# Where the tiles of an encoder trunk begin in SBUF: small tiles first, large tiles at multiples of 256 bytes

## The chip, the cores and the metric

The kernel runs on one core of a Trainium2 chip. The metric is the device time of one execution in microseconds (us). Before the change the median of three runs is 1626.02 us (1625.46 to 1627.36).

## What is computed

One layer of a bidirectional encoder on 256 rows (tokens) of 2048 channels, all in float32. A combined input projection feeds a gated short convolution and a grouped-query attention (16 query heads, 4 key/value heads of 128 channels, two-dimensional rotary positions); both are projected, gated, merged and projected once more. Then comes a squared-ReLU MLP with 8192 hidden channels. RMS norms stand before and after each half.

```python
h = rmsnorm(x, norm_mix_pre[l])
z = h @ w_in[l]
conv_b, conv_c, conv_in, q, k, v, g_a, g_b = jnp.split(z, IN_OFFSETS, axis=-1)
y_a = short_conv_mixer(conv_b, conv_c, conv_in, conv_w[l], w_out_conv[l])
...
y_b = block_gqa(q, k, v) @ w_out_attn[l]
...
mixed = (gate_a * y_a + gate_b * y_b) @ w_merge[l]
x = x + rmsnorm(mixed, norm_mix_post[l])
h = rmsnorm(x, norm_mlp_pre[l])
f = jnp.square(jax.nn.relu(h @ w_up[l])) @ w_down[l]
x = x + rmsnorm(f, norm_mlp_post[l])
```

## The kernel before

Almost all the work is matrix products of the 256 activations with weight matrices that are read once from HBM. A weight matrix is cut into blocks of 512 columns; a block is read in granules of two K tiles (128 partitions x 2 x 512 float32, 512 KB, tile `raw`, queue SP, L121). `split` (L72) turns a granule into two fp32r tiles: ScalarE rounds it (`whi`, L75), VectorE subtracts that from the original (`wlo`, L76). The activations lie split in the same way in SBUF: `pair` (L83) makes one tile `A`, `B` or `C` of 32 KB in each partition that holds the rounded part and the remainder, 16 K tiles of 256 rows each. Three matmuls then make one product: high x high, one part's high with the other's remainder, and the reverse.

There are two forms of the product:

- `linear_channels` (L161): the weights are stationary (128 columns of `whi` or `wlo`), the activations move, 256 columns a matmul (L175, L179, L182). A granule has 24 matmuls. The gated convolution, the gates, both branch projections and 15 of the 16 up-projection blocks run so.
- `linear` (L133): the activations are stationary, the weights move, 512 columns a matmul (L145, L146, L147). A granule has 12 matmuls. K, V, the four Q blocks, the merge, the first up-projection block and the whole down projection run so.

Attention proper (L377 to L379) uses the same triple of 256 columns: scores have `qh` or `ql` stationary and `kh`/`kl` (tile `kv`) moving; values have `vh`/`vl` (tile `kv`) stationary and the probabilities `ph`/`pl` moving. TensorE also transposes (L224, L410, L575), with the 128x128 identity `ident` moving.

The order of the work is written out by hand: small pieces are put off by a number of granules (`later`, `tick`). The granules of one block follow each other without a gap in the program.

Two rings hold `whi` and `wlo`. While attention and convolution run (up to about 450 us) there is the pool `wts` alone, four tiles of each. After that the pool `wts2` takes the place of the mixing stage's tiles, and `weights` (L113) changes between the rings every four granules:

```python
pool = rings[count[0] // WB % len(rings)]
count[0] += 1
```

A pool takes a consecutive piece of each partition in the order in which the pools are opened (L61 to L70), and each tile in it a place that is rounded up to 32 bytes. Before the change the small tiles of `const` (1184 bytes) come first, then `big`, `wts`, `wk`, the small tiles of `sm` (704 bytes), and last the pool of the mixing stage, whose place `wts2` and `late` take over. The start of each tile in its partition, in bytes:

```
tiles                                  before          start modulo 256
ident                                  16512           128
A / kv, m, mg / C / B      17696, 50464, 66848, 99616   32
raw, whi, wlo of wts               132384 to 181535     32
bias, cc (and what shares its place)   181536 ...       32
mixing stage: ph, pl, qh, ql, z, ra    190432 ...      224
whi, wlo of wts2                       190432 ...      224
```

Rows, K tiles and column blocks inside these tiles are 512, 1024 or 2048 bytes apart, so every operand of a matmul begins at the same remainder as its tile.

Of the kernel before, what the change touches and what calls it, by code (L numbers as in the profile page):

```python
# [9 lines left out]
F32 = mybir.dt.float32  # L10
# [5 lines left out]
P = 128  # L16
D = 2048
T = 256
NT = T // P
# [13 lines left out]
def trunk_kernel(  # L33
# [16 lines left out]
    nc = tc.nc  # L50
# [8 lines left out]
    WARM = 9  # L59

    const = ctx.enter_context(tc.tile_pool(name="const", bufs=1))  # L61
    big = ctx.enter_context(tc.tile_pool(name="big", bufs=1))
    wts = ctx.enter_context(tc.tile_pool(name="wts", bufs=WB))
    wk = ctx.enter_context(tc.tile_pool(name="wk", bufs=2))
    sm = ctx.enter_context(tc.tile_pool(name="sm", bufs=2))
    ps_acc = ctx.enter_context(tc.tile_pool(name="ps_acc", bufs=4, space=bass.MemoryType.PSUM))
    ps_tr = ctx.enter_context(tc.tile_pool(name="ps_tr", bufs=2, space=bass.MemoryType.PSUM))
    ps_at = ctx.enter_context(tc.tile_pool(name="ps_at", bufs=2, space=bass.MemoryType.PSUM))
# [64 lines left out]
    def linear(act, wv, done, k0=0, k1=KT, lag=0, ahead=None):  # L133

        ah, al, _ = act
        accs = [ps_acc.tile([P, CH], F32, name="acc") for _ in range(NT)]

        def step(t, k, wh, wl):  # L140
            ts_ = slice(t * P, (t + 1) * P)
            for g in range(KG):
                a = k - k0 + g
                first, last = a == 0, a == k1 - k0 - 1
                nc.tensor.matmul(accs[t], lhsT=ah[:, a, ts_], rhs=wh[:, g, :], start=first, stop=False)  # L145
                nc.tensor.matmul(accs[t], lhsT=ah[:, a, ts_], rhs=wl[:, g, :], start=False, stop=False)  # L146
                nc.tensor.matmul(accs[t], lhsT=al[:, a, ts_], rhs=wh[:, g, :], start=False, stop=last)  # L147
            if k + KG == k1:
                done(t, accs[t])

        behind = []
        for gran in weights(wv, k0, k1, ahead):
            behind.append(gran)
            step(0, *gran)
            if len(behind) > lag:
                step(1, *behind.pop(0))
            tick()
        for gran in behind:
            step(1, *gran)
# [42 lines left out]
    def along_rows(dst, cols):  # L202

        rb = ps_at.tile([P, T], F32, name="at")
        ones = wk.tile([P, P], F32, tag="cc", bufs=CCB, name="ones")
        nc.vector.memset(ones, 1.0)
        for t in range(NT):
            diag = wk.tile([P, P], F32, tag="cc", bufs=CCB, name="diag")
            nc.vector.tensor_scalar_mul(diag, ident, cols[t])
            nc.tensor.matmul(rb[:, t * P : (t + 1) * P], lhsT=ones, rhs=diag, start=True, stop=True)  # L210
        nc.vector.tensor_copy(dst, rb)
# [20 lines left out]
    def rsqrt_mean(dst, ss, n):  # L232

        ms = sm.tile(list(ss.shape), F32, name="ms")
        nc.vector.tensor_scalar(ms, ss, 1.0 / n, EPS, op0=ALU.mult, op1=ALU.add)
        nc.gpsimd.tensor_tensor(dst, ms, mhalf.broadcast_to(list(ss.shape)), op=ALU.pow)  # L236

    def row_squares(dst, src):

        junk = wk.tile([P, CH], F32, tag="cc", bufs=CCB, name="junk")  # L240
        nc.scalar.activation(junk, src, AF.Square, accum_out=dst)

    def total(dst, parts):

        s = sm.tile([P, NT], F32, name="tot")
        nc.vector.tensor_reduce(s, parts, axis=AX.X, op=ALU.add)
        rsqrt_mean(dst, s, D)
# [10 lines left out]
        nc.scalar.activation(act, zero[:, :1], AF.Square)  # L258
    ident = const.tile([P, P], F32, name="ident")
    make_identity(nc, ident)  # L260
    mhalf = const.tile([P, 1], F32, name="mhalf")
    nc.vector.memset(mhalf, -0.5)
    ch = const.tile([P, 7, KT], F32, name="ch")
    nc.scalar.dma_start(ch, chan)
    g_pre, g_mlp, cw = ch[:, 0, :], ch[:, 1, :], ch[:, 2:5, :]
# [7 lines left out]
        for i in range(n):  # L273
            split(xt[:, i, :], hT[0][:, k + i, :], hT[1][:, k + i, :], scale=g_pre[:, k + i : k + i + 1])

    rstd = const.tile([P, NT], F32, name="rstd")
    norm_row = wk.tile([P, 2, T], F32, name="bias", bufs=1)
    xv = x.rearrange("(t p) d -> p t d", p=P)
    tabs = [mx.tile([P, 2, NT, HD], F32, name=f"tab{i}", bufs=1) for i in range(2)]

    def norm_in():

        ss0 = const.tile([P, NT, 4], F32, name="ss0")
        for j in range(4):
            xj = mx.tile([P, NT, CH], F32, tag="t4", bufs=4, name="xj")
            nc.sync.dma_start(xj, xv[:, :, j * CH : (j + 1) * CH])
            for t in range(NT):
                row_squares(ss0[:, t, j : j + 1], xj[:, t, :])
        total(rstd, ss0)
        along_rows(norm_row[:, 0, :], [rstd[:, t : t + 1] for t in range(NT)])  # L290
        nc.vector.tensor_tensor(norm_row[:, 1, :], norm_row[:, 0, :], norm_row[:, 0, :], op=ALU.mult)
# [71 lines left out]
    kl = kv[:, 1]  # L363
    later(9, tables)
    later(11, norm_in)
    head_norm_rope(w_in[C_K], tabs[1], kh, kl, 7, wait=6, ahead=first_operands)
    vh = kv[:, 2].rearrange("p a b -> p (a b)").rearrange("p (t c) -> p t c", t=NT)
# [160 lines left out]
    def gain_row(r):  # L528
        g = wk.tile([P, CH], F32, name="bias", bufs=1)
        nc.scalar.dma_start(g, rows[r : r + 1, :].partition_broadcast(P))  # L530
        return g
# [1 line left out]
    rows1 = const.tile([P, 6], F32, name="rows1")  # L533

    def row_rsqrt(parts, t, at):
        s = sm.tile([P, 1], F32, name="s1")
        nc.vector.tensor_reduce(s, parts[:, t, :], axis=AX.X, op=ALU.add)
        r = rows1[:, at : at + 1]
        rsqrt_mean(r, s, D)
        return r  # L540


    ss1 = const.tile([P, NT, 4], F32, name="ss1")
    ss2 = const.tile([P, NT, 4], F32, name="ss2")
    xr = big.tile([P, 2, NT, D], F32, tag="A", name="xr")[:, 0]
    nc.scalar.dma_start(xr, xv)
# [18 lines left out]
    def residual(t, x2):  # L565
        r = row_rsqrt(ss1, t, t)
        ts_ = slice(t * P, (t + 1) * P)
        for c in range(4):
            cs = slice(c * CH, (c + 1) * CH)
            nc.vector.scalar_tensor_tensor(x2[:, t, cs], x2[:, t, cs], r, xr[:, t, cs], op0=ALU.mult, op1=ALU.add)  # L570
            pool, name = bank(c)
            tr = pool.tile([P, 4, P], F32, name=name)
            for i in range(4):
                d = c * 4 + i
                nc.tensor.transpose(tr[:, i, :], x2[:, t, d * P : (d + 1) * P], ident)  # L575
            ds = slice(c * 4, c * 4 + 4)
            n = wk.tile([P, 4, P], F32, tag="cc", bufs=CCB, name="cc")
            nc.vector.tensor_tensor(n, tr, g_mlp[:, ds].unsqueeze(2).broadcast_to([P, 4, P]), op=ALU.mult)
            split(n, x2T[0][:, ds, ts_], x2T[1][:, ds, ts_])
# [8 lines left out]
    def norms():  # L588
        for t in range(NT):
            for j in range(4):  # L590
                row_squares(ss2[:, t, j : j + 1], x2[:, t, j * CH : (j + 1) * CH])
            rstd2[t] = row_rsqrt(ss2, t, 2 + t)
        along_rows(rstd2_row, rstd2)
# [36 lines left out]
    before = [None] * NT  # L630

    def finish(t, last):
        ms = sm.tile([P, 1], F32, name="ms3")
        nc.vector.scalar_tensor_tensor(ms, ss3[:, t, 3:4], 1.0 / D, before[t], op0=ALU.mult, op1=ALU.add)
        r = sm.tile([P, 1], F32, name="rs3")
        nc.gpsimd.tensor_tensor(r, ms, mhalf, op=ALU.pow)
        for c in range(4):
            js = slice(c * CH, (c + 1) * CH)
            f = facc[:, t, js] if c < 3 else last
            nc.vector.scalar_tensor_tensor(x2[:, t, js], f, r, x2[:, t, js], op0=ALU.mult, op1=ALU.add)  # L640
            nc.sync.dma_start(outv[:, t, js], x2[:, t, js])

    def down(q, j, fT):
        js = slice(j * CH, (j + 1) * CH)
        g = gain_row(4 + j) if q == 3 else None

        def done(t, acc):
            fj = facc[:, t, js]
            if q == 0:
                nc.scalar.copy(fj, acc)  # L650
                return
            nc.vector.tensor_tensor(fj, acc, fj, op=ALU.add)
            if q < 3:
                return
            row_squares(ss3[:, t, j : j + 1], fj)
            if j < 3:
                nc.vector.tensor_tensor(fj, fj, g, op=ALU.mult)
            else:
                last = wk.tile([P, CH], F32, tag="cc", bufs=CCB, name="cc")
                nc.vector.tensor_tensor(last, fj, g, op=ALU.mult)  # L660
                finish(t, last)
            if j == 2:
                s = sm.tile([P, 1], F32, name="s1")
                nc.vector.tensor_reduce(s, ss3[:, t, :3], axis=AX.X, op=ALU.add)
                before[t] = rows1[:, 4 + t : 5 + t]
                nc.vector.tensor_scalar(before[t], s, 1.0 / D, EPS, op0=ALU.mult, op1=ALU.add)

        linear(fT, w_dn[j], done, q * KT, (q + 1) * KT, lag=LAG if q == 3 and j == 3 else 0)
# [71 lines left out]
```

## Time and profile before

| what | value |
|---|---|
| median of three runs | 1626.02 us (1625.46 to 1627.36) |
| the profiled execution, its own time | 1625.61 us |
| its span, from first to last instruction | 1623.8 us |
| TensorE matmul busy | 1610.9 us, 99% of the span |
| VectorE, ScalarE, GpSimd busy | 947.5, 709.5, 35.6 us |
| read from HBM | 302.44 MB, 188 GB/s over the span |

The profile is one execution taken by the hardware profiler. The span is cut into 40 slices for a row of digits that gives busy shares in tenths. A matmul's duration in the trace runs from its start to its end through the array, and neighbours overlap; what a matmul costs in a row of them is the distance from one start to the next. The view by stretches counts every instruction that is under way in the stretch, so at its edges it counts one to three more than begin in it.

### The profile page before, as it was taken

The page shows a single profiled execution, that of the slowest core. Times are in us where ns is not written, and L with a number is a line of the kernel's source. Part 1 is how long each engine was busy: PE and PEld are TensorE (multiplying, and loading weights), DVE is VectorE, ACT ScalarE, POOL GpSimd, SP SyncE. Part 2 cuts the span into 40 slices and gives each one's busy share as a digit, 9 for nine tenths or more (in the row PEclk, how much of TensorE's full clock was granted, in tenths as well). Part 3 has the DMA queues.
Part 4 walks back from the last instruction along what each step waited for, and adds up shares of the span by engine and source line. Part 5 has one row for each costly group of instructions (what it writes and reads, how often), then busy time and mean ns, then how long its engine had stood idle before and what let it go on. Part 6 is the DMA issues. An engine that isn't in the chain of part 4 may idle for free.

```text
span 1623.8 us, 26863 instructions
## 1 busy us (share of the span) xinstructions
PE 1610.9 (99%) x11210; PEld 1497.9 (92%) x11210; DVE 947.5 (58%) x1107; ACT 709.5 (44%) x860; POOL 35.6 (2%) x23
## 2 busy tenths in 40 slices
PE   9999999999999999999999999999999999999997
PEld 7899999999999999999988898889988998899986
DVE  6767676576764544555554865446654565555654
ACT  7444444444454443444444644444433344333441
POOL 0210101001000000000000000000000000000000
PEclk9999999999999999999999999999999999999999
DMA  8654545555475556565765566555565565556562
GB/s 317 204 177 156 181 147 181 181 167 183 149 241 186 186 188 194 186 190 184 243 204 177 172 209 195 189 187 189 185 197 189 187 190 189 193 182 195 191 200 83
DMA packets 86297, 306.28 MB, mean 189 GB/s; under 512 B 9632, under 2 KB 10016, under 8 KB 85920
## 3 DMA queue, kind: packets, MB, share of 16 engines
q1 hardware_dynamic: 84608, 300.32, 57.2%
q10 hardware_dynamic: 1568, 4.25, 0.8%
q8 instruction: 87, 1.43, 0.4%
q14 instruction: 34, 0.28, 0.1%
HBM read 302.44 MB, written 2.10 MB: 188 GB/s over the span
## 4 chain that ended last, share of the span: by engine, by line
PE 97%; DVE 1%; issue 1%; DMA 0%; POOL 0%; ACT 0%; SPq 0%; DVEq 0%; POOLq 0%; ACTq 0%
PE acc L182 20%; PE acc L175 20%; PE acc L179 20%; PE acc L146 12%; PE acc L147 12%; PE acc L145 12%; PE at L377 0%; PE at L379 0%; PE at L378 0%; PE tr L410 0%; DMA raw<-in_w_in 0%; PE tr L224 0%; POOL rs L236 0%; DVE wlo L76 0%; PE tr L575 0%
## 5 line engine op out<-in xcount | busy, mean ns | idle before, releaser
L76 DVE TENSOR_TENSOR wlo<-raw,whi 128x1024 fp32r<-128x1024 f32 (+1 forms) x561 | 684.2, 1221 | 602.8 <-ACT whi L75 590.9
L75 ACT CAST whi<-raw 128x1024 fp32r<-128x1024 f32 (+1 forms) x561 | 587.1, 1048 | 774.2 <-PE acc L179 401.6
L175 PE MATMUL acc<-A,whi 128*128 128x256 f32 x1280 | 362.3, 283 | 0.0
L182 PE MATMUL acc<-A,wlo 128*128 128x256 f32 x1280 | 360.4, 282 | 0.0
L179 PE MATMUL acc<-A,whi 128*128 128x256 f32 x1280 | 360.3, 282 | 0.0
L175 PE MATMUL acc<-C,whi 128*128 128x256 f32 x1216 | 340.0, 280 | 0.0
L182 PE MATMUL acc<-C,wlo 128*128 128x256 f32 x1216 | 339.9, 280 | 0.0
L179 PE MATMUL acc<-C,whi 128*128 128x256 f32 x1216 | 339.9, 279 | 0.0
L145 PE MATMUL acc<-whi,A 128*128 128x512 f32 x704 | 275.0, 392 | 2.2 <-ACT whi L75 2.2
L146 PE MATMUL acc<-wlo,A 128*128 128x512 f32 x704 | 275.9, 392 | 1.0 <-DVE wlo L76 1.0
L147 PE MATMUL acc<-whi,A 128*128 128x512 f32 x704 | 275.3, 391 | 0.0
L179 PEld LDWEIGHTS acc<-A,whi 128*128 128x128 f32 x1280 | 244.4, 191 | 0.2
L175 PEld LDWEIGHTS acc<-A,whi 128*128 128x128 f32 x1280 | 244.4, 191 | 0.2
L182 PEld LDWEIGHTS acc<-A,wlo 128*128 128x128 f32 x1280 | 244.5, 191 | 0.0
L175 PEld LDWEIGHTS acc<-C,whi 128*128 128x128 f32 x1216 | 230.8, 190 | 0.2
L179 PEld LDWEIGHTS acc<-C,whi 128*128 128x128 f32 x1216 | 230.8, 190 | 0.2
L182 PEld LDWEIGHTS acc<-C,wlo 128*128 128x128 f32 x1216 | 230.8, 190 | 0.0
L145 PEld LDWEIGHTS acc<-whi,A 128*128 128x128 f32 x704 | 131.8, 188 | 32.1 <-ACT whi L75 3.1
L146 PEld LDWEIGHTS acc<-wlo,A 128*128 128x128 f32 x704 | 132.0, 187 | 31.9 <-DVE wlo L76 2.7
L147 PEld LDWEIGHTS acc<-whi,A 128*128 128x128 f32 x704 | 132.0, 187 | 29.0
L182 PE MATMUL acc<-B,wlo 128*128 128x256 f32 x256 | 71.6, 280 | 0.0
L179 PE MATMUL acc<-B,whi 128*128 128x256 f32 x256 | 71.6, 280 | 0.0
(144 smaller groups left out, 1115.6 us busy)
## 6 DMA issues: line engine op xcount, KB each, us to landing
raw<-in_w_in SPq DMA_DIRECT2D x207, 512.0 KB, 4.3
raw<-in_w_up SPq DMA_DIRECT2D x128, 512.0 KB, 3.5
raw<-in_w_dn SPq DMA_DIRECT2D x128, 512.0 KB, 3.4
raw<-in_w_oc SPq DMA_DIRECT2D x32, 512.0 KB, 4.4
raw<-in_w_oa SPq DMA_DIRECT2D x32, 512.0 KB, 4.3
raw<-in_w_mg SPq DMA_DIRECT2D x32, 512.0 KB, 4.1
xj<-in_x SPq DMA_DIRECT2D x4, 512.0 KB, 9.0
xr<-in_x ACTq DMA_DIRECT2D x1, 2048.0 KB, 9.7
```

The costliest lines, as they stand in the source:

```text
L75: nc.scalar.copy(hi, src)
L76: nc.vector.tensor_tensor(lo, src, hi.bitcast(F32), op=ALU.subtract)
L145: nc.tensor.matmul(accs[t], lhsT=ah[:, a, ts_], rhs=wh[:, g, :], start=first, stop=False)
L146: nc.tensor.matmul(accs[t], lhsT=ah[:, a, ts_], rhs=wl[:, g, :], start=False, stop=False)
L147: nc.tensor.matmul(accs[t], lhsT=al[:, a, ts_], rhs=wh[:, g, :], start=False, stop=last)
L175: nc.tensor.matmul(acc, lhsT=wh[:, g, cs], rhs=ah[:, a, :], start=a == 0 and c % 2 == 0, stop=False, skip_group_check=True,)
L179: nc.tensor.matmul(acc, lhsT=wh[:, g, cs], rhs=al[:, a, :], start=False, stop=False, skip_group_check=True)
L182: nc.tensor.matmul(acc, lhsT=wl[:, g, cs], rhs=ah[:, a, :], start=False, stop=a == KT - 1, skip_group_check=True)
```

## The change

The pool `sm` is opened right after `const`, ahead of `big`. Some small tiles are merged or share a place: `ss0` and `ss1` become halves of `ss01`, `mhalf` and `rstd` columns of `half`, and `s1`, `ms3`, `rs3` take turns in the places of `rden`, `ms`, `rs`. The small tiles then end at byte 18176, which is 71 x 256; all later tiles are multiples of 256 bytes long. So `A` begins at 18176, `kv` at 50944, `C` at 67328, `B` at 100096, `raw` at 132864, the `whi`/`wlo` of `wts` at 149248 and on, and the mixing stage's tiles and `wts2` at 190208: all at remainder 0. `ident` stays at 16512.

```diff
     const = ctx.enter_context(tc.tile_pool(name="const", bufs=1))
+
+    sm = ctx.enter_context(tc.tile_pool(name="sm", bufs=2))
     big = ctx.enter_context(tc.tile_pool(name="big", bufs=1))
     wts = ctx.enter_context(tc.tile_pool(name="wts", bufs=WB))
     wk = ctx.enter_context(tc.tile_pool(name="wk", bufs=2))
-    sm = ctx.enter_context(tc.tile_pool(name="sm", bufs=2))
...
-    mhalf = const.tile([P, 1], F32, name="mhalf")
-    nc.vector.memset(mhalf, -0.5)
+    ss01 = const.tile([P, 2, NT, 4], F32, name="ss01")
+    half = const.tile([P, 4], F32, name="half")
+    nc.vector.memset(half, -0.5)
+    mhalf = half[:, :1]
+    rstd = half[:, 2:4]
...
-    rstd = const.tile([P, NT], F32, name="rstd")
...
-        ss0 = const.tile([P, NT, 4], F32, name="ss0")
+        ss0 = ss01[:, 0]
...
-        s = sm.tile([P, 1], F32, name="s1")
+        s = sm.tile([P, 1], F32, tag="rden", name="s1")
...
-    ss1 = const.tile([P, NT, 4], F32, name="ss1")
+    ss1 = ss01[:, 1]
...
-        ms = sm.tile([P, 1], F32, name="ms3")
+        ms = sm.tile([P, 1], F32, tag="ms", name="ms3")
...
-        r = sm.tile([P, 1], F32, name="rs3")
+        r = sm.tile([P, 1], F32, tag="rs", name="rs3")
...
-                s = sm.tile([P, 1], F32, name="s1")
+                s = sm.tile([P, 1], F32, tag="rden", name="s1")
```

No instruction moves: on every engine the same instructions stand in the same order, with the same waits on all but GpSimd. GpSimd has one more wait ahead of each of its last two instructions (L636 before, in `finish`).

## Rows read from the trace of the kernel before

**Rows 1.** The page: busy time by engine, the slices of TensorE and its clock.
```profile
PE 1610.9 (99%) x11210; PEld 1497.9 (92%) x11210; DVE 947.5 (58%) x1107; ACT 709.5 (44%) x860; POOL 35.6 (2%) x23
PE   9999999999999999999999999999999999999997
...
PEclk9999999999999999999999999999999999999999
```

**Rows 2.** The page: the chain that ended last, share of the span by engine.
```profile
PE 97%; DVE 1%; issue 1%; DMA 0%; POOL 0%; ACT 0%; SPq 0%; DVEq 0%; POOLq 0%; ACTq 0%
```

**Rows 3.** Groups by line and shape: line, engine, operation, tiles, count, busy us, mean ns.
```profile
L175 PE MATMUL acc<-A,whi 128*128 128x256 f32 x1280 | 362.3, 283 | 0.0
L175 PE MATMUL acc<-C,whi 128*128 128x256 f32 x1216 | 340.0, 280 | 0.0
L175 PE MATMUL acc<-B,whi 128*128 128x256 f32 x256 | 71.6, 280 | 0.0
...
L145 PE MATMUL acc<-whi,A 128*128 128x512 f32 x704 | 275.0, 392 | 2.2 <-ACT whi L75 2.2
L145 PE MATMUL acc<-whi,B 128*128 128x512 f32 x128 | 50.2, 392 | 0.0
L145 PE MATMUL acc<-whi,C 128*128 128x512 f32 x32 | 12.5, 396 | 0.0
L410 PE MATMUL tr<-ident,pr 128*128 128x128 f32 x64 | 9.6, 273 | 0.0
```

**Rows 4.** Timeline of TensorE where a ring of weights ends: start us, us, instruction.
```profile
461.97 0.28 PE L175 MATMUL acc<-A,whi 128*128 128x256 f32 x1
462.09 0.28 PE L179 MATMUL acc<-A,whi 128*128 128x256 f32 x1
462.21 0.28 PE L182 MATMUL acc<-A,wlo 128*128 128x256 f32 x1
462.33 0.28 PE L175 MATMUL acc<-A,whi 128*128 128x256 f32 x1
462.44 0.28 PE L179 MATMUL acc<-A,whi 128*128 128x256 f32 x1
462.56 0.28 PE L182 MATMUL acc<-A,wlo 128*128 128x256 f32 x1
462.67 0.28 PE L175 MATMUL acc<-A,whi 128*128 128x256 f32 x1
```

**Rows 5.** TensorE by stretches: us, busy (count), granted clock, DMA share, GB/s.
```profile
139.43:153.81 14.38, 14.38 (x122) 1.00 0.73 239
153.81:175.60 21.79, 21.79 (x99) 1.00 0.60 191
462.33:473.21 10.88, 10.88 (x98) 1.00 0.81 272
473.21:484.73 11.52, 11.52 (x98) 1.00 0.70 241
1003.78:1014.98 11.20, 11.20 (x50) 1.00 0.59 190
1014.98:1025.88 10.90, 10.90 (x50) 1.00 0.60 195
```

**Rows 6.** Timeline of TensorE in attention: values, then scores, then a block.
```profile
121.06 0.28 PE L377 MATMUL at<-ph,kv 128*128 128x256 f32 x1
121.18 0.28 PE L378 MATMUL at<-pl,kv 128*128 128x256 f32 x1
121.29 0.28 PE L379 MATMUL at<-ph,kv 128*128 128x256 f32 x1
121.40 0.28 PE L377 MATMUL at<-kv,qh 128*128 128x256 f32 x1
...
122.08 0.28 PE L175 MATMUL acc<-A,whi 128*128 128x256 f32 x1
```

**Rows 7.** Timeline of TensorE: four transposes of attention, merged into one row.
```profile
113.37 0.60 PE L410 MATMUL tr<-ident,pr 128*128 128x128 f32 x4
```

**Rows 8.** All engines by stretches (PE, PEld, DVE, ACT, POOL): the start of the kernel.
```profile
15.00:50.00 35.00, 35.00 (x157) 28.91 (x156) 26.46 (x52) 23.64 (x39) 5.04 (x2) 1.00 0.81 290
```

**Rows 9.** Timeline of GpSimd at the end: what it does and what it waited for.
```profile
1610.34 0.54 POOL L636 TENSOR_TENSOR rs<-ms,mhalf 128x1 f32<-128x1 f32 x1 [690.08 <-DVE ms L634]
1617.32 0.54 POOL L636 TENSOR_TENSOR rs<-ms,mhalf 128x1 f32<-128x1 f32 x1 [6.44 <-DVE ms L634]
```

## Prediction

> **What bounds the kernel now.** I read the page first. [...] The chain that ended last is TensorE for 97% [rows 2]. So the time is the sum of TensorE's matmuls, one after the other, and other engines and transfers count only where they make it wait. The next question is what one matmul costs in a row of them, and whether it costs the same everywhere. It does not.
>
> The timeline shows a change in the middle of a block: up to 462.33 us matmuls of 256 columns start 0.12 us apart, after it 0.11 to 0.12 in turn [rows 4]. Nothing waits there, the lines and shapes are the same; what changes is the ring from which the weights come. The stretches make it exact [rows 5]. The 96 matmuls of four granules take 10.88 us with weights from the second ring, 113.3 ns each, and 11.52 us with weights from the first, 120.0 ns. In the mixing stage, where there is only the first ring, 120 matmuls (five granules) take 14.38 us, 119.8 ns. The form with 512 columns differs too, and the other way round: 48 matmuls take 11.20 us with the second ring, 233.3 ns, and 10.90 with the first, 227.1; the 96 of a Q block take 21.79 us, 227.0 (first ring).
>
> The rings differ in where they begin: the first at 32 past a multiple of 256 bytes, the second at 224 past. The activations (A, B, C) always begin at 32 past. Attention confirms that it is not the ring as such: scores, with qh at 224 past and keys at 32 past, run at 0.11 to 0.12, and so do the values once they have begun, with probabilities at 224 past against vh at 32 past [rows 6].
>
> [...]
>
> **The change part by part.** The program is the same on TensorE, instruction by instruction; only starts move. Afterwards every large operand begins at a multiple of 256, so both operands of a matmul begin at the same remainder, as in today's first ring (32 and 32), but without the odd 32 bytes. [...]
>
> I take one unit less than the first ring has. [...] That gives 113.3 ns for 256 columns and 220.0 for 512, in both rings.
>
> - Weights stationary: three lines of 1280 + 1216 + 256 = 2752 make 8256 matmuls [rows 3]. The mixing stage has 12 blocks of 192, 2304, all from the first ring. The other 5952 (31 blocks) are half and half. First ring: 2304 + 2976 = 5280 x 6.67 ns = **35.2 us** less. Second ring: 2976 stay at 113.3, **0**.
> - Weights moving: 704 + 128 + 32 = 864 on each of three lines, 2592 [rows 3]. Six blocks of 96 lie in the mixing stage, 21 after it. Of the six, K and V (192) fall in the first 70 us, where transfers and splits set the pace for much of the time [rows 8], so I count them at nothing; at most they give 1.3 us. First ring: 384 + 1008 = 1392 x 6.67 = **9.3 us** less. Second ring: 1008 x 13.33 = **13.4 us** less.
> - Attention's own 192 matmuls, the transposes (ident does not move) and PSUM: **0**; at most 192 x 6.67, 1.3 us.
> - The weights' landing places: no row has a landing at a multiple of 256. [...] I take **0**.
> - VectorE and ScalarE: hidden behind TensorE; at 58% of the span [rows 1] VectorE would stand at 60% of 1568 us, so the cover holds. **0**.
> - Shared places: ms3, rs3 and s1 wait for tenants that finished long ago; GpSimd had idled 690 us when L636 came [rows 9]. Two extra waits of GpSimd stand in the last norm, the second on the path to the end. One should cost less than the 0.54 us of the instruction behind it; I take **0.1 us** more, bounds 0 and 0.54.
>
> Sum: 35.2 + 9.3 + 13.4 - 0.1 = 57.8 us less. From the profiled execution's own 1625.6 that is 1567.8; the median of the runs, 1626.0, stands 0.4 above it. I predict **1568 us**. If the form with 512 columns keeps its two units and only sheds the third, the gain is 35.2 + 1008 x 6.67 = 41.9 and the time 1584: the same case with its smaller size. Its own range is 1560 to 1587.
>
> **Rivals.**
>
> [...]
>
> [...]
>
> *The difference of the two starts counts, not the starts.* Weights are loaded while activations move; if two reads get in each other's way by their distance modulo 256, then making all starts equal makes every matmul what the first ring is today. The second ring's stationary weights go from 113.3 to 120.0, 2976 x 6.67 = 19.8 us more, its moving weights from 233.3 to 227, 6.7 less: 13.1 us slower, 1639. It decides if equal starts at remainder 0 cost as much as at 32. For it: with 256 columns both unequal pairs (scores and values) are faster than the equal one [rows 6]. [...]
>
> *The change does not reach what it aims at.* The second ring also lies elsewhere: from byte 190432 on, the first below 181536. If the region counts and not the remainder, nothing moves by more than 480 bytes and the alternation stays: 1626. Against it: one region would have to help 256 columns and hurt 512.
>
> [...]
>
> **How the numbers follow.** Forecast with its smaller size 0.45; all excess gone 0.27; differences count 0.15; no effect 0.13. A measurement of this kernel can tell some 0.2% (3 us) from no change. So faster 0.72, same 0.13, slower 0.15. The range reaches from 1510, which holds the likelier part of the first rival (1521), up to 1629, which takes in no effect; it leaves out the slower case and the end at 1497, under 2 in 10. It is wide because a price that no row shows is multiplied by 10656.
>
> **What would show it.** Right: the start-to-start distance is 113 ns for 256 columns and 220 for 512, and no longer changes every four granules; the mean of L175 falls to about 276 ns for A, B and C; the chain stays at 97% TensorE. [...] Differences count: 120 and 227 throughout. No effect: the alternation stays. My reasoning would be wrong altogether if the distances matched the forecast but the time did not, since then TensorE would wait for transfers or splits that it covers today.

## The result, and the profile after

The change makes the kernel slower: 1640.63 us median (1639.69 to 1641.41, four runs) against 1626.56 before (1625.46 to 1627.36), a ratio of 1.0087, 95% interval 1.0069 to 1.0104. The forecast was 1568; the rival in which the difference of the two starts counts gave 1639.

On the page nothing has changed but the amount: TensorE fills the span and is the chain, at the same clock, a mean of 0.997 granted against 0.999 before [rows 1, 2].

```profile
span 1639.3 us, 26865 instructions
PE 1626.6 (99%) x11210; PEld 1520.9 (93%) x11210; DVE 947.5 (58%) x1107; ACT 710.0 (43%) x860; POOL 35.6 (2%) x23
...
PE 98%; DVE 1%; DMA 0%; POOL 0%; issue 0%; ACT 0%; SPq 0%; DVEq 0%; POOLq 0%; ACTq 0%
```

The groups by shape answer to [rows 3]; the lines stand one lower or more in the changed file (L175 is now L176, L145 is L146). Before, the 256-column groups of `C` and `B`, which the two rings share half and half, had a mean of 280 ns and that of `A`, with the mixing stage in it, 283. Now `C` and `B` are at 283 and `A` at 285. The 512-column group of `B` went the other way, from 392 to 389.

```profile
L176 PE MATMUL acc<-A,whi 128*128 128x256 f32 x1280 | 364.2, 285 | 0.0
L176 PE MATMUL acc<-C,whi 128*128 128x256 f32 x1216 | 344.3, 283 | 0.0
...
L176 PE MATMUL acc<-B,whi 128*128 128x256 f32 x256 | 72.4, 283 | 0.0
L146 PE MATMUL acc<-whi,B 128*128 128x512 f32 x128 | 49.8, 389 | 0.0
```

TensorE by stretches of the changed kernel answers to [rows 5]. The first two rows are the 96 matmuls (256 columns) of four granules from the first ring and of the next four from the second; the last two are 48 matmuls (512 columns) from the second ring and then the first.

```profile
476.24:487.76 11.52, 11.52 (x98) 1.00 0.65 207
487.76:499.28 11.52, 11.52 (x98) 1.00 0.62 186
1016.93:1027.81 10.88, 10.88 (x49) 1.00 0.68 204
1027.81:1038.69 10.88, 10.88 (x49) 1.00 0.67 197
```

The rings no longer differ: 11.52 / 96 = 120.0 ns and 10.88 / 48 = 226.7 ns in both. The pair that had 113.3 ns is gone, and so is the one at 233.3. The span grew by 15.4 us. 2976 matmuls at +6.67 ns are 19.8 us, 1008 at -6.67 are -6.7; attention's 192, which went from 22.14 to 23.03 us (115.3 to 119.9 ns each), add 0.9. Together that is 14.0, and the medians differ by 14.1. The other 1.4 us are a difference of the two traced executions: they arose in the first 20 us, where 62 matmuls were under way against 68 before and TensorE's granted clock was 0.91 against 1.00. The rows are the first 15 us before, then the first 15 and the next 35 us after (the next 35 us before: [rows 8]).

```profile
0.00:15.00 15.00, 11.24 (x46) 1.00 0.82 298
0.00:15.00 15.00, 11.62 (x42) 0.90 0.86 295
15.00:50.00 35.00, 35.00 (x156) 0.99 0.78 280
```

### The profile page after: what moved, and what is told of

It reads as the page before. It is cut to its first block, busy times and chain, and to the rows that moved or that the text cites. A ratio compares the mean times of both kernels' runs of the same rounds, so it can differ in the third digit from the quotient of the medians.

```text
span 1639.3 us, 26865 instructions
## 1 busy us (share of the span) xinstructions
PE 1626.6 (99%) x11210; PEld 1520.9 (93%) x11210; DVE 947.5 (58%) x1107; ACT 710.0 (43%) x860; POOL 35.6 (2%) x23
## 3 DMA queue, kind: packets, MB, share of 16 engines
q10 hardware_dynamic: 1568, 4.25, 0.8%
## 4 chain that ended last, share of the span: by engine, by line
PE 98%; DVE 1%; DMA 0%; POOL 0%; issue 0%; ACT 0%; SPq 0%; DVEq 0%; POOLq 0%; ACTq 0%
PE acc L183 20%; PE acc L176 20%; PE acc L180 20%; PE acc L147 12%; PE acc L148 12%; PE acc L146 12%; PE at L381 0%; PE at L380 0%; PE at L382 0%; PE tr L413 0%; DMA raw<-in_w_in 0%; PE tr L225 0%; POOL rs L237 0%; DVE wlo L77 0%; PE tr L578 0%
## 5 line engine op out<-in xcount | busy, mean ns | idle before, releaser
L176 PE MATMUL acc<-A,whi 128*128 128x256 f32 x1280 | 364.2, 285 | 0.0
L176 PE MATMUL acc<-C,whi 128*128 128x256 f32 x1216 | 344.3, 283 | 0.0
L183 PE MATMUL acc<-C,wlo 128*128 128x256 f32 x1216 | 344.1, 283 | 0.0
L180 PE MATMUL acc<-C,whi 128*128 128x256 f32 x1216 | 344.1, 283 | 0.0
L146 PE MATMUL acc<-whi,A 128*128 128x512 f32 x704 | 274.3, 391 | 1.8 <-ACT whi L76 1.8
L176 PEld LDWEIGHTS acc<-A,whi 128*128 128x128 f32 x1280 | 245.7, 192 | 0.2
L180 PEld LDWEIGHTS acc<-C,whi 128*128 128x128 f32 x1216 | 233.4, 192 | 0.2
L176 PEld LDWEIGHTS acc<-C,whi 128*128 128x128 f32 x1216 | 233.4, 192 | 0.2
L183 PEld LDWEIGHTS acc<-C,wlo 128*128 128x128 f32 x1216 | 233.4, 192 | 0.0
L146 PEld LDWEIGHTS acc<-whi,A 128*128 128x128 f32 x704 | 132.5, 189 | 29.8 <-ACT whi L76 2.7
L176 PE MATMUL acc<-B,whi 128*128 128x256 f32 x256 | 72.4, 283 | 0.0
L180 PE MATMUL acc<-B,whi 128*128 128x256 f32 x256 | 72.4, 283 | 0.0
```

The costliest lines, as they stand in the source:

```text
L176: nc.tensor.matmul(acc, lhsT=wh[:, g, cs], rhs=ah[:, a, :], start=a == 0 and c % 2 == 0, stop=False, skip_group_check=True,)
L180: nc.tensor.matmul(acc, lhsT=wh[:, g, cs], rhs=al[:, a, :], start=False, stop=False, skip_group_check=True)
L183: nc.tensor.matmul(acc, lhsT=wl[:, g, cs], rhs=ah[:, a, :], start=False, stop=a == KT - 1, skip_group_check=True)
```

## The experiments

All kernels below are the changed one with unused bytes put between pools, unless something else is said. "Distance" is the start of the activations minus that of the weights, modulo 256; for the 512-column form, where the weights move, the distance of moving minus stationary operand is its negative. Spacings are a stretch's time divided by its matmuls.

### Other distances

```diff
     big = ctx.enter_context(tc.tile_pool(name="big", bufs=1))
+    pad1 = ctx.enter_context(tc.tile_pool(name="pad1", bufs=1)).tile([P, 8], F32, name="pad1")
     wts = ctx.enter_context(tc.tile_pool(name="wts", bufs=WB))
     wk = ctx.enter_context(tc.tile_pool(name="wk", bufs=2))
+    pad2 = ctx.enter_context(tc.tile_pool(name="pad2", bufs=1)).tile([P, 8], F32, name="pad2")
```

The first pad was 32, 96, 160 or 224 bytes, the second 32 (none in the last). Two theories were on record: D, that the distance alone counts, and O, that each operand's own remainder counts.

Rings at 32 and 64:

> The changed kernel with 32 unused bytes ahead of the first ring of weights and 32 more ahead of the second: activations begin at remainder 0 (modulo 256), the first ring at 32, the second at 64. Theory D (the distance between the starts of the two operands modulo 256 counts, nothing else): the distances 32 and 64 are other than 0, so both rings leave the 120.0 ns (256 columns) and 226.7 ns (512 columns) that the changed kernel has throughout; the second ring's distance of -64 (activations minus weights) was not in the trace of before, the two signs need not be alike. Theory O (each operand's own remainder counts, and 224 is the special one): no operand is at 224, so 120.0 and 226.7 throughout and about 1641 us.

Rings at 96 and 128:

> As the run before, with the first ring at remainder 96 and the second at 128, activations at 0. [...] Theory O: 120.0 and 226.7 throughout, about 1641 us.

Rings at 160 and 192:

> First ring at remainder 160, second at 192, activations at 0. The second ring has the distance that it had before the change (activations minus weights is 64 modulo 256), at other remainders (0 and 192 in place of 32 and 224). Theory D: its spacings come back, 113.3 ns for 256 columns and 233.3 ns for 512; that alone is 2976 x 6.67 less and 1008 x 6.67 more, 13.1 us under the changed kernel's 1641; the first ring (distance 96) is new. Theory O: 120.0 and 226.7 throughout, about 1641 us.

Both rings at 224:

> Both rings at remainder 224, activations at 0, so one distance, 32 (activations minus weights). Theory O (224 is special): the spacings of the second ring of before, 113.3 and 233.3 ns, everywhere: 8256 matmuls 6.67 ns shorter and 2592 that much longer than 120.0 and 226.7, so 1641 - 55.1 + 17.3 = 1603 us. Theory D: one pair of spacings for all, that of distance 32, which no run has shown yet, and no alternation every four granules.

Measured, one run each below the first row, the kernel before at 1627.3 beside them. The spacings are those that most stretches have in the gates and branch projections (256 columns, from about 470 us on) and in the down projection (512 columns):

| rings at | time, us | 256 columns, first / second ring, ns | 512 columns, first / second, ns |
|---|---|---|---|
| 0, 0 (the change) | 1640.6 | 120.0 / 120.0 | 226.7 / 226.7 |
| 32, 64 | 1623.9 | 118.3 / 113.3 | 233.2 / 228.8 |
| 96, 128 | 1641.6 | 117.3 / 118.6 | 233.3 / 233.2 |
| 160, 192 | 1645.7 | 120.0 / 117.7 | 234 / 233.3 |
| 224, 224 | 1627.9 | 116.7 / 116.7 | 233.3 / 233.3 |

The stretches that show it best are those of 160 and 192 (first ring, then second):

```profile
478.83:490.35 11.52, 11.52 (x99) 1.00 0.68 219
490.35:501.65 11.30, 11.30 (x98) 1.00 0.63 188
```

with the second ring again in the up projection,

```profile
1108.80:1119.69 10.89, 10.89 (x99) 1.00 0.62 195
```

and those of 224 for both rings (256 columns twice, then 512):

```profile
469.51:480.71 11.20, 11.20 (x98) 1.00 0.74 245
480.71:491.91 11.20, 11.20 (x98) 1.00 0.63 189
816.70:827.90 11.20, 11.20 (x49) 1.00 0.65 198
```

Theory O falls: it held that the spacings stay at 120.0 and 226.7 in the first three kernels, and that the last one runs at 113.3 and 1603 us. Theory D holds as far as the spacing changes with the distance, between 113.3 and 120.0 ns and between 226.7 and 234 in the table. One number of it missed. The second ring at 192 has the distance of before (64), and its 512-column form is at 233.3 as expected, but its 256-column form settles in most stretches at 11.30 / 96 = 117.7 ns and at 113.4 only in the last three quarters of the up projection. With the first ring's 512-column form at 234 ns in place of 226.7, the time went up to 1645.7, where 13.1 us less were expected from the second ring alone. So a distance need not have one spacing. The ring at 96 shows the same: 117.3 ns in the gates and branches, 118.6 to 118.8 in most of the later up projection.

### One part undone

```diff
+    pad2 = ctx.enter_context(tc.tile_pool(name="pad2", bufs=1)).tile([P, 48], F32, name="pad2")
     ps_acc = ctx.enter_context(tc.tile_pool(name="ps_acc", bufs=4, space=bass.MemoryType.PSUM))
```

> The changed kernel with one part undone: 192 unused bytes ahead of the mixing stage's pool, so that the second ring (and qh, ph of attention) stand again at the distance that they had before from the activations (64 modulo 256), at remainder 192. The small tiles stay first and shared, the first ring stays at 0. Theory D (the distance between the two operands' starts costs, not the shared small tiles): the alternation of before comes back, 113.3 and 233.3 ns in the second ring, and the time of before: 1640.6 - 19.8 - 0.6 + 6.7, about 1627 us. Theory S (shared places and the order of the pools cost something of their own): it stays above 1630.

Measured: 1625.49 us median of ten runs against 1625.90, ratio 0.9997, interval 0.9987 to 1.0006. The alternation is back (first ring, second ring with 256 columns; second, first with 512):

```profile
473.26:484.78 11.52, 11.52 (x98) 1.00 0.69 227
484.78:495.66 10.88, 10.88 (x98) 1.00 0.64 195
1003.86:1015.06 11.20, 11.20 (x50) 1.00 0.60 192
1015.06:1025.96 10.90, 10.90 (x50) 1.00 0.61 195
```

They are the four spacings of [rows 5], 120.0, 113.3, 233.3 and 227.1, with the activations and the first ring at remainder 0 and not 32. That shows three things. The whole loss of the change lies in where the second ring and the mixing stage's tiles stand. The shared small tiles and the new order of the pools cost nothing that can be measured. And at equal distances the 32 odd bytes cost nothing, so taking them away gains nothing.

### The two reads by themselves

Groups of 48 matmuls were added at the end, where nothing else runs on TensorE:

```diff
+    def probe(n, mov, stat, m=P):
+        acc = ps_tr.tile([P, CH], F32, name="tr")
+        for i in range(REP):
+            nc.tensor.matmul(
+                acc[:m, :n],
+                lhsT=af[:, 2048 + stat // 4 : 2048 + stat // 4 + m],
+                rhs=cf[:, 1024 + mov // 4 : 1024 + mov // 4 + n],
+                start=i == 0, stop=i == REP - 1, skip_group_check=True,
+            )
```

> The changed kernel with 30 groups of 48 matmuls added at its end, all on one line, whose results go nowhere: they read pieces of tile A as stationary and of tile C as moving operand, at chosen starts. Nothing else runs on TensorE then. Groups: 256 and 512 columns at 16 distances in steps of 16 bytes; 256 columns with the stationary operand shifted by 32, 64, 192, 224 instead; stationary operands of 64 and 32 columns; 128 moving columns. Theory D: at distance 0 the groups run at 120.0 and 226.7 ns, at other distances at others; where the stationary operand is shifted by x, 256 columns run as where the moving one is shifted by 256 - x. [...]

TensorE by stretches, each from the first start of a group to the last, 47 spacings. In order: 256 columns with the moving operand at 0, 96, 112, 192 and 64 past the stationary one; 256 columns with the stationary operand shifted by 192 (distance 64 again); 512 columns at 0 and 32; 256 and 512 columns at 0 with 32 stationary columns; 256 columns with the moving operand at 32 and then, instead, the stationary one shifted by 224 (distance 32 again); 512 columns at 240.

```profile
1629.82:1635.45 5.63, 5.63 (x48) 1.00 0.28 108
1663.97:1669.61 5.64, 5.64 (x49) 1.00 0.00 0
1669.73:1675.06 5.33, 5.33 (x50) 1.00 0.00 0
1697.90:1703.24 5.34, 5.34 (x49) 1.00 0.00 0
1652.56:1658.10 5.54, 5.54 (x50) 1.00 0.00 0
1909.67:1914.99 5.32, 5.32 (x49) 1.00 0.01 3
1720.39:1731.09 10.70, 10.70 (x50) 1.00 0.00 0
1742.43:1753.40 10.97, 10.97 (x48) 1.00 0.01 1
1937.46:1942.79 5.33, 5.33 (x49) 1.00 0.02 3
1953.94:1964.83 10.89, 10.89 (x49) 1.00 0.00 0
1641.28:1646.76 5.48, 5.48 (x49) 1.00 0.01 3
1915.11:1920.59 5.48, 5.48 (x49) 1.00 0.00 0
1887.66:1898.32 10.66, 10.66 (x48) 1.00 0.01 2
```

The spacings are 119.8, 120.0, 113.4, 113.6, 117.9; 113.2; 227.7 and 233.4; 113.4 and 231.7; 116.6 twice; 226.8 ns. The first group still runs beside the last norm and its stores (DMA share 0.28); behind them the program has no work left for VectorE and ScalarE, and the DMA share is 0.00 to 0.02. The effect is the same, so it needs nothing but TensorE's own work on the two operands. Sixteen bytes decide (120.0 ns at 96, 113.4 at 112). Distance 64 shows both 117.9 and 113.2. Taking three quarters of the stationary columns away changes the spacing though the moving read is the same, from 119.8 to 113.4 with 256 columns and from 227.7 up to 231.7 with 512: the size of the stationary operand takes part. Whether it is its load was not separated, since the output has fewer rows then too. The best groups of 256 columns are at 113.2 to 113.6 ns, and the one at distance 192, where both starts are multiples of 64, is among them.

Other sizes, the state before a group, and bfloat16 were tried in a second probe:

> The changed kernel with 25 groups of 48 matmuls added at its end as in the earlier run, one line, nothing else on TensorE. Groups: 192, 256, 320, 384, 448, 512 moving columns at distance 192 and at distance 0; 256 and 512 with 32 stationary columns at distance 192; 256 columns at distances 0, 64, 192, 64, 64 in this order (entered from different states); 256 and 512 columns of bfloat16 at distances 0, 32, 64. [...] Theory P (two settled states at distance 64, chosen by the state before): the group at 64 after one at 0 settles at 117.8, the one at 64 after one at 192 at 113.3; otherwise both alike.

Its stretches: 256 columns at distance 64, entered after a group at distance 0, and after one at distance 192; bfloat16 with 256 columns at distances 0 and 32; bfloat16 with 512 columns at 0.

```profile
1746.51:1752.05 5.54, 5.54 (x50) 1.00 0.01 3
1757.61:1762.94 5.33, 5.33 (x49) 1.00 0.00 0
1768.71:1773.85 5.14, 5.14 (x49) 1.00 0.00 0
1773.96:1779.09 5.13, 5.13 (x49) 1.00 0.00 0
1784.44:1794.59 10.15, 10.15 (x50) 1.00 0.00 0
```

117.9 against 113.4 ns at one and the same distance, as theory P had it. But P is not shown: a third group at distance 64, after the one at 113.4, was at 117.8, and in the kernels the rule fails. Where one ring is at distance 0 and the other at 64 (the kernel before, and the kernel with one part undone), the second ring follows distance 0 every time, and its stretches after the mixing stage are all at 113.3, not 117.8 [rows 5]. What chooses the spacing stays open. Bfloat16 is at 109.4, 109.1 and 216.0, and with 256 columns the distances tried do not differ by more than that: the groups at 32 and 64 together take 10.48 us (1773.96 to 1784.44), 109.2 ns for each of 96 matmuls. That is below the lowest of float32r, 113.2 and 226.7; which of the things in which the two types differ counts is not shown. Of the sizes, 320 columns took 146.7 ns at both distances and 384 took 173.4 at distance 0, while 448 took 206.7 there and 202.1 at distance 192.

### Versions that use the distance

Both rings at 64, so distance 192 for the 256-column form, the larger one, everywhere:

```diff
+    pad1 = ctx.enter_context(tc.tile_pool(name="pad1", bufs=1)).tile([P, 16], F32, name="pad1")
     wts = ctx.enter_context(tc.tile_pool(name="wts", bufs=WB))
```

> Both rings at remainder 64, activations at 0. In the second ring of an earlier run (activations 0, weights 64) most matmuls of 256 columns ran at 113.3 ns and some stretches at 117.8, and 512 columns at 230.1. Theory D with that: if the better state holds throughout, 8448 matmuls gain 6.67 ns and 2592 lose 3.4: 1640.6 - 56.3 + 8.8 = 1593 us. If the stretches settle at 117.8 it is 1640.6 - 18.6 + 8.8 = 1631 us; in any case faster than the changed kernel.

One run: 1593.9 us, as expected for the better state. Its 256-column stretches after the mixing stage, first and second ring, and one of 512 columns:

```profile
463.05:473.93 10.88, 10.88 (x98) 1.00 0.76 256
473.93:484.81 10.88, 10.88 (x98) 1.00 0.63 196
1003.87:1014.85 10.98, 10.98 (x49) 1.00 0.58 191
```

113.3, 113.3 and 228.8 ns. The same kernel was then timed, on another occasion:

> The same kernel as the run with both rings at 64 and the activations at 0, now timed. Theory P (two settled states at distances 64 and 192, 113.3 and 117.8 ns, chosen by the state before, the same in every execution): again 1594 us in each. If the choice differs between executions, the times spread from 1594 to about 1620.

1608.05 us median (1607.49 to 1609.46, four runs) against 1627.07, ratio 0.9887, interval 0.9870 to 0.9903. Better than both kernels, and not 1594. The stretches say why: the gates and branch projections had settled at 11.30 / 96 = 117.7 ns, the up projection at 113.3.

```profile
462.24:473.54 11.30, 11.30 (x98) 1.00 0.73 236
...
940.92:951.80 10.88, 10.88 (x99) 1.00 0.60 188
```

So the spacing is not fixed by the program alone. The four runs of the second occasion agreed within 2 us; the first was one run, on another chip (3, then 9). The chip alone cannot decide, since one trace can hold both spacings, as this one does. What else differed between the two occasions is not known.

The remainders of the old second ring for all weights (activations at 32, both rings at 224; 32 unused bytes ahead of `big`, 192 ahead of `wts`):

> The changed kernel with 32 unused bytes ahead of the activations and 192 more ahead of the rings: activations at 32, both rings at 224, the very remainders of the second ring before the change, now for all weights. Theory D: 113.3 ns for all 8448 matmuls of 256 columns (56.3 us less than the changed kernel) and 233.3 for the 2592 of 512 (17.3 more): 1640.6 - 56.3 + 17.3 = 1602 us; up to 1640 where the stretches settle at 117.8.

One run, 1620.8 us: between the two ends. The gates and branch projections are at 113.3 ns, the up projection at 117.8:

```profile
468.78:479.66 10.88, 10.88 (x98) 1.00 0.78 266
1081.58:1092.89 11.31, 11.31 (x99) 1.00 0.61 188
```

All starts 32 bytes further at the distance of the best run (activations at 32, rings at 96):

> The same with everything from the activations on 32 bytes further: activations at 32, both rings at 96, the distance unchanged. Theory D (the distance alone): the settled spacings are again 113.3 or 117.8 ns for 256 columns and about 229 to 233 for 512, none of 120.0 or 226.7, and the time lies between 1594 and 1630 us. If starts at odd multiples of 32 cost a unit of their own (the step of the prediction), it is 8448 + 2592 units of 6.67 ns more than the run before: over 1660 us.

1617.70 us median of four, ratio 0.9941 (0.9926 to 0.9956): the gates at 117.8, most of the up projection at 113.3, no 120.0 and no 226.7. The odd 32 bytes cost no unit; 1660 is far off.

```profile
457.41:468.71 11.30, 11.30 (x98) 1.00 0.88 289
1093.45:1104.33 10.88, 10.88 (x98) 1.00 0.63 194
```

Last, a distance for each form. Tile `A` gets a pool of its own ahead of the rings, and the down projection's activations begin 64 bytes into it:

```diff
+    def pair_a(at):
+        n = 2 * KT * T
+        whole = biga.tile([P, n + 16], F32R, tag="A", name="A")
+        return views(whole[:, at : at + n].rearrange("p (a k t) -> p a k t", a=2, k=KT))
...
-    hT = pair("A")
+    hT = pair_a(0)
...
-        fT = pair("A")
+        fT = pair_a(16)
```

> Both rings at remainder 64 as in the run with 64 and 64, activations at 0, but tile A lies in a pool of its own right ahead of the rings, 64 bytes longer, and the hidden activations of the down projection begin 64 bytes into it, so that there the two operands begin alike (distance 0). Theory D: 256 columns stay at 113.3 ns after the mixing stage, and the 1536 matmuls of the down projection go from about 230.1 to 227 ns, 4.8 us less than the 1594 us of that run: 1589 us, 36 to 37 us under the kernel before. If the spacing belonged to the code's form and not to the distance, it stays at 1594.

1617.86 us median (1613.76 to 1619.25), ratio 0.9938, interval 0.9924 to 0.9951: not the 1589 expected. Three stretches split the answer: a block of the gates and one of the up projection (192 matmuls, 256 columns each), and the quarter of the down projection ahead of the latter (384 matmuls, 512 columns):

```profile
495.00:517.60 22.60, 22.60 (x194) 1.00 0.59 183
1254.00:1276.60 22.60, 22.60 (x194) 1.00 0.58 186
1166.90:1254.00 87.10, 87.10 (x387) 1.00 0.60 193
```

The down projection came to 87.10 / 384 = 226.8 ns, as the distance says. But the gates and branch projections, ahead of any down projection, are at 22.60 / 192 = 117.7 ns and not at 113.3, as in the timed run of both rings at 64. Their 3072 matmuls make the larger part of the miss, some 13.6 us. After each quarter of the down projection the up projection settles at 117.7 too, some 10 us on 2304 matmuls, where its blocks ahead of the first quarter are at 113.3. That is more than the 3 us that the down projection gained over 228.8 ns. The five runs lie 5.5 us apart, more than the 2.4 of the kernel before beside them, so the spacings may differ between executions as well; only one of the five was traced.

## Why the prediction was wrong

- **What bounds the kernel** was right: TensorE back to back, at a granted clock of 1.00 in the stretches, and the time is a sum of spacings. The spacings and counts carried over: 19.8 and -6.7 us were in the text, in the sum of the rival on the difference of the two starts.
- **The step that failed** is "I take one unit less than the first ring has". The unit of the sum is 6.67 ns, the difference between 120.0 and 113.3; that it goes with the odd 32 bytes was the author's estimate, and no run shows such a term. Measured, 32 bytes past and 0 past cost the same at the same distance: 120.0 and 226.7 ns in the changed kernel, 120.0 and 227.1 before, and the old alternation came back at remainders 0 and 192. Moving everything by 32 bytes at distance 192 cost no unit either, 113.3 and 117.8 ns before it and after. The unit that was to go stayed in both rings of the changed kernel. The 35.2 and the 9.3 us of the sum were therefore 0. Nor does any run show 220.0 ns, or the units that the smaller size of 1584 us counts: 512 columns of float32r stand at 226.7 ns or more in all the rows above.
- **The second ring's terms** follow from the same step. The prediction had the second ring become what the first ring is, less one unit. It did become what the first ring is, but the unit stayed: its 113.3 ns, which it had by its distance, turned into 120.0, and a term of 0 became +19.8 us. Of the 13.4 us for its 512-column form half was right, 6.7, because 233.3 fell to the level of equal starts, 226.7. One unit on all 10656 matmuls is 71.0 us, almost the whole gap between 1568 and 1640.6.
- **The rival that held**, the difference of the starts, had 1639 us and a chance of 0.15, and the range left it out; 1640.6 was measured. What spoke against it, the slower unequal pair with 512 columns (233.3 against 227.1 ns [rows 5]), only says that a distance acts on each form in its own way, as the probe found: from distance 0 to 32, 256 columns went from 119.8 to 116.6 ns and 512 from 227.7 to 233.4. The rows of attention, two pairs with unequal starts and both fast, were the better evidence and were already in hand [rows 6].
- **All excess gone** has a chance of 0.27, and 1521 and 1497 us in the range. No run shows the terms behind these times: float32r stayed at 113.2 to 120.0 ns with 256 columns and at 226.7 to 234 with 512. The bfloat16 groups were lower, 109.1 to 109.4 and 216.0.
- **The change does not reach what it aims at**: excluded by the changed kernel itself, whose second ring lies in the old region and lost its alternation.
- **The terms of 0** (transfers, splits, shared places, GpSimd's two waits) are confirmed together by the kernel with one part undone, at a ratio of 0.9997. Attention's 0 was not: its unequal pairs became equal and cost 0.9 us more (22.14 to 23.03 us).

## What to carry to other kernels

When equal instructions take different times in different stretches of one trace, sort them by the addresses of their operands, pairwise and not one by one, before explaining the difference by alignment: here it was a relation, and making all starts alike put every matmul of 256 columns at the slower spacing, 120.0 ns. A forecast for an address that no row shows should go by a probe with chosen starts, which took some 350 and 180 us of a run here. For float32r matmuls with both operands in SBUF the distance of the two starts modulo 256 is worth a try of a few paddings, but the gain is to be timed on several occasions, since one distance can settle in more than one way (113.3 and 117.8 ns at 64 and 192).

## What the runs showed of the hardware

- Float32r matmuls back to back depend on the distance between the starts of their two operands: 120.0 ns at 0 and 96, 116.7 at 32, 113.4 at 112, 113.3 or 117.8 at 64 and 192 with 256 columns; 226.7 (227.7 in the probe) at 0, 226.8 at 240 and 228.8 to 234 at the other distances tried with 512. That the distance counts modulo 256 is supported by a pair that differs by 256 bytes: shifting the stationary operand by 224 or the moving one by 32 gave 116.6 both ways. Why the distance counts, and where the two reads would meet, was not shown.
- At distances 64 and 192, 256 columns have two settled spacings, 113.3 and 117.8 ns, and long stretches of one trace keep one of them. What chooses is open: the same program chose differently on two occasions, 1594 and 1608 us, and after distance 0 both were seen, 113.3 in the kernel before and 117.9 in the probe.
- Bfloat16 showed none of this at the distances tried with 256 columns: 109.4 ns at 0, 109.1 at 32, 109.2 for 32 and 64 together.
